# Sums of W_out built during the first pair's output projection, and one form of the branch kept in DRAM

## The chip, the cores and the metric

The kernel runs on one core of a Trainium2 chip. Its engines work side by side, each through its own list of instructions and strictly in that order: TensorE (PE, with its weight loads as PEld), VectorE (DVE), ScalarE (ACT), GpSimd (POOL) and SyncE (SP), which here only issues DMAs. POOL and ScalarE can issue DMAs too. The metric is the device time in microseconds; less is better.

## The reference

One layer of an encoder trunk over 2048 rows of 1024 numbers, in fp32. Cut to what matters here:

```python
hn = rms_norm(h, norm_g[i])
proj = jnp.einsum('bsd,de->bse', hn, pool_w_in[j])
u, mq, gate = jnp.split(proj, [POOL_WIDTH, POOL_WIDTH + MEM_WIDTH], axis=-1)
tok = multi_scale_pool(u, w_group[j], scale[j])
mem_o = memory_attention(mq, mem_k, mem_v)
branch = jnp.concatenate([tok, mem_o], axis=-1) * jax.nn.silu(gate)
h = h + jnp.einsum('bse,ed->bsd', branch, w_out[i])
return rms_norm(h, final_norm_g)
```

## The kernel before, in words

The rows are handled in two pairs of blocks, 1024 rows each; pair 0 first. Each pair goes through an input projection (queries, gates, pooled columns, with the attention to the memory spread between the products) and an output projection. Every matrix product of fp32 numbers is made of three matmuls on a high part and a low part (`_mm3`, L51 to L53): `_split` (L42) makes the parts, the high one by a cast on ScalarE (L38), the low one by a subtraction on VectorE (L46). `chunk` (L411) does this for weights, into a ring of four buffers `wh` and `wl`.

Pair 1 uses seven products of quarter matrices in place of eight, in both projections. So sums and differences ("forms") of quarters are needed: of its inputs (X1), of its branch (Y, seven forms) and of W_out (four forms, 5, 6, 7 and 4).

- `stage_weights(k)` (L702), for k = 0 to 3, makes the sums of W_out: four loads of 256 KB, four subtractions on VectorE (`combine`, L241, whose operations are recorded at L102), and four stores of 256 KB to `t_d` by POOL's queue (L714). Before, it works in three `zz` buffers (a ring of four that the queries and the pooling use as well) and an `sg` buffer, loads by SP (L708), and is called inside the second pair's input projection, `project_in(1)`, after products 12, 26, 30 and 34 of its 56.
- `stage_branch(k)` (L674) makes the forms of pair 1's branch: it loads two pieces of the branch (`load_branch`, L645: from `br_d`, or, for the attention's, from `o_d` with its gate from `g_d`, multiplied at L655), adds and subtracts on VectorE (L102, L105), and either splits a form into its slots (Y) or stores it to `ys_d` (L690). Its buffers are `raw`, a ring of four that the weight chunks use as well. It is called in `project_out(0)`, the first pair's output projection, at the chunks (dh, c) = (0, 2), (0, 3), (1, 0) and (1, 1).
- `y_later(p)` (L694) loads a stored form again and splits it into slots.
- `project_out(0)` (L774): for each half dh of the columns, four chunks c of W_out (load at L780, 512 KB), 48 matmuls each into eight PSUM banks; after the half, `Rows.complete` (L744) adds the banks into h on VectorE (L742).
- `project_out_by_products` (L802): seven products of 48 matmuls, in the order 1, 2, 6, 7, 5, 4, 3; products 5, 6, 7 and 4 load their weights from `t_d` (L817).

Large slots x0 to x13 (`slot`, L84) hold X1, the split branch of pair 0 and Y in turn, one tile at a time; a new tile of a slot waits for every use of the old one. x6 and x7 hold form 4 of X1 during `project_in(1)`, and form 6 of Y after it.

The listing sets the rank of each instruction; a planner that runs a model of time then orders each engine's list by rank and by when buffers and operands come free in that model. So loads of a later stage can be issued well before the stage, and an instruction on the chip waits at the place in the list that the planner gave it. What it waits for is set by the tiles: POOL's, SP's and ScalarE's DMAs wait in their engine's list.

Of the kernel before, what the change touches and what calls it, by code (L numbers as in the profile page):

```python
# [8 lines left out]
F32 = mybir.dt.float32  # L9
# [6 lines left out]
P = 128  # L16
# [3 lines left out]
KH = KT // 2  # L20
BT = 512
# [35 lines left out]
def trunk(ctx, tc, x, xT, mem, memT, norm_g, mem_norm_g, w_mem, w_out, w_in, w_uT, w_g, p_scale, final_g,  # L57
# [5 lines left out]
    nc = tc.nc  # L63
    sp = nc.sync
# [8 lines left out]
    sgp = pool("sgp", 2)  # L73
# [5 lines left out]
    dram = pool("dram", 1, space=bass.MemoryType.DRAM)  # L79
# [4 lines left out]
    def slot(n, shape=(P, KH, BT), dt=F32R):  # L84
        return sl.tile(list(shape), dt, name=f"x{n}")

    def zz(shape, dt=F32):

        n = 1
        for v in shape[1:]:  # L90
            n *= v
        t = zw.tile([P, HALO + D], dt, name="zz")[:, :n]
        if len(shape) == 3:
            t = t.rearrange("p (a b) -> p a b", a=shape[1])
        return t
# [566 lines left out]


    YPLACE = {1: (2, 3), 2: (4, 5), 6: (6, 7), 7: (8, 9), 5: (10, 11), 4: (12, 13), 3: (0, 1)}
    ys_d = dram.tile([KH, P, 4, BT], F32, name="ys_d")
    t_d = dram.tile([4, 2, P, 2, BT], F32, name="t_d")
    LATER = (7, 5, 4, 3)
    FORMS = (5, 6, 7, 4)
    Y = {}

# [2 lines left out]

    def stage_branch(k):  # L674
        if not Y:
            for p in (1, 2, 6):
                y_slots(p)
        r = [load_branch(1, e, lambda: raw_tile((P, 2, BT))) for e in (k, k + KH)]
        a11, a21, a12, a22 = r[0][:, 0, :], r[0][:, 1, :], r[1][:, 0, :], r[1][:, 1, :]
        t = raw_tile((P, 2, BT))  # L680
        s1, s2 = t[:, 0, :], t[:, 1, :]
        s4 = st.tile([P, BT], F32, name="s")
        g = nc.vector
        add(g, s1, a21, a22)
        sub(g, s2, s1, a11)
        sub(g, a21, a11, a21)
        sub(g, s4, a12, s2)
        for p, v in {1: a11, 2: a12, 6: s2, 7: a21, 5: s1, 4: a22, 3: s4}.items():
            if p in LATER:
                sp.dma_start(out=ys_d[k, :, LATER.index(p), :], in_=v)  # L690
            else:
                _split(nc, Y[p][0][:, k, :], Y[p][1][:, k, :], v, "act")

    def y_later(p):  # L694
        y_slots(p)
        for k in range(0, KH, 2):
            rt = raw_tile((P, 2, BT))
            sp.dma_start(out=rt, in_=ys_d[k:k + 2, :, LATER.index(p), :].rearrange("k p t -> p k t"))
            for kk in range(2):
                _split(nc, Y[p][0][:, k + kk, :], Y[p][1][:, k + kk, :], rt[:, kk, :], "act")  # L700

    def stage_weights(k):  # L702

        r = []
        for kk in (k, k + KH):
            r.append(zz((P, 2, BT)))
            for dh in range(2):
                sp.dma_start(out=r[-1][:, dh, :], in_=w_out[kk // 2, dh, :, kk % 2, :])  # L708
        t = zz((P, 2, BT))
        t4 = sgp.tile([P, BT], F32, name="sg")  # L710
        b11, b12, b21, b22 = r[0][:, 0, :], r[0][:, 1, :], r[1][:, 0, :], r[1][:, 1, :]
        combine(b11, b12, b21, b22, t[:, 0, :], t[:, 1, :], t4)
        for i, v in enumerate((t[:, 0, :], t[:, 1, :], b12, t4)):
            nc.gpsimd.dma_start(out=t_d[i, k // 2, :, k % 2, :], in_=v)  # L714
# [59 lines left out]
    def project_out(s, bh, bl, between):  # L774
        rows = Rows(s)
        for dh in range(2):
            pss = [pl.tile([P, BT], F32, name=n) for pl, n in [(ps_mm, "mm")] * 4 + [(ps_s, "sc")] * 2 + [(ps_t, "pt")] * 2]
            for c in range(4):
                wr = raw_tile((P, 2, BT))
                sp.dma_start(out=wr, in_=w_out[c, dh])  # L780
                ws = [chunk(wr[:, kk, :], "act") for kk in range(2)]
                if dh == 0 and c == 2:
                    rows.load()
                between(dh, c)

                rounds = [[(kk, t)] for kk in range(2) for t in range(NT)]
                if c == 3:
                    rounds = [[(kk, t) for kk in range(2)] for t in range(NT)]
                for todo in rounds:
                    for kk, t in todo:  # L790
                        e = 2 * c + kk
                        tk = slice(t % QT * P, (t % QT + 1) * P)
                        ah, al = bh[t // QT, e // KH], bl[t // QT, e // KH]
                        _mm3(nc, pss[t], ah[:, e % KH, tk], al[:, e % KH, tk], ws[kk][0], ws[kk][1], e == 0, e == KT - 1)
            for t in range(NT):
                added = rows.complete(t, dh, pss[t])
                if dh and t:
                    with tc.issue_after(added.ins):
                        rows.finish(t - 1)
        rows.finish(NT - 1)  # L800

    def project_out_by_products():  # L802
        rows = Rows(1)
        banks = {}

        def product(p, onto=None, tile_by_tile=False, each=None):
            if onto:
                banks[p] = banks[onto]
            elif p == 1:
                banks[p] = [ps_mm.tile([P, BT], F32, name="mm") for _ in range(QT)]  # L810
            else:
                banks[p] = [pl.tile([P, BT], F32, name=n) for pl, n in ((ps_s, "sc"), (ps_t, "pt")) for _ in range(2)]
            ws = []
            for c in range(2):
                wr = raw_tile((P, 2, BT))
                if p in FORMS:
                    sp.dma_start(out=wr, in_=t_d[FORMS.index(p), c])  # L817
                else:
                    sp.dma_start(out=wr, in_=w_out[c + 2 * (p > 1), int(p == 3)])
                ws += [chunk(wr[:, kk, :], "act") for kk in range(2)]  # L820
            order = [(k, t) for k in range(KH) for t in range(QT)]
            if tile_by_tile:
                order = [(k, t) for t in range(QT) for k in range(KH)]
            for k, t in order:
                tk = slice(t * P, (t + 1) * P)
                _mm3(nc, banks[p][t], Y[p][0][:, k, tk], Y[p][1][:, k, tk], ws[k][0], ws[k][1], k == 0 and not onto,
                     k == KH - 1, skip_group_check=onto is not None)
                if tile_by_tile and k == KH - 1:
                    each(t)

        def all_tiles(p, f, t0, dh):
            for t in range(QT):
                f(t0 + t, dh, banks[p][t])

        product(1)
        rows.load()
        all_tiles(1, rows.add, 0, 0)
        product(2)
        all_tiles(2, rows.complete, 0, 0)
        y_later(7)  # L840
        product(6, 1)
        all_tiles(6, rows.add, QT, 0)
        y_later(5)
        product(7)
        all_tiles(7, rows.add, QT, 1)
        y_later(4)
        product(5, 6)
        all_tiles(5, rows.complete, QT, 1)
        y_later(3)
        product(4, 7)  # L850
        for t in range(QT):
            added = rows.complete(QT + t, 0, banks[4][t])
            if t:
                with tc.issue_after(added.ins):
                    rows.finish(QT + t - 1)
        rows.finish(2 * QT - 1)

        def last(t):
            added = rows.complete(t, 1, banks[5][t])
            if t:  # L860
                with tc.issue_after(added.ins):
                    rows.finish(t - 1)
        product(3, 5, True, last)
        rows.finish(QT - 1)
# [46 lines left out]
    def norm(a):  # L911
        first_norm(a)
        for f in unscaled[a]:
            f()

    hooks = {7: [lambda: norm(0)], 10: [lambda: norm(1)], 11: [load_fold] * 4 + [lambda: loaded.extend(load_memory())],
             12: [fold, lambda: ahead.append(load_tile(w_in[6], load))],
             14: [lambda: load_memory_rest(loaded)],
             15: [lambda: memory_norm(loaded)], 17: [lambda: memory(loaded)], 19: [lambda: stats(0)], 21: [lambda: stats(1)]}
# [23 lines left out]
    bhl = [({}, {}), ({}, {})]  # L943
# [11 lines left out]
            branch(s, e, *bhl[s], lambda: (zz if by == "zz" else raw_tile)((P, 2, BT)))  # L955

    hooks = {NP - 4: [lambda: bring(0, 0, (0, 1, 2, 3), "zz")], NP - 2: [lambda: bring(0, 1, (4, 5, 6, 7), "zz")]}
    for k, n in enumerate((12, 26, 30, 34)):
        hooks[n] = [lambda k=k: stage_weights(k)]
    project_in(1, X1, Steps(1, 10, 2, hooks))  # L960

    AT_CHUNK = {(0, 2): 0, (0, 3): 1, (1, 0): 2, (1, 1): 3}
    project_out(0, *bhl[0], lambda dh, c: stage_branch(AT_CHUNK[dh, c]) if (dh, c) in AT_CHUNK else None)
    project_out_by_products()


# [47 lines left out]
```

## Time and profile before

| | us |
|---|---|
| median of 3 runs | 629.32 (629.0 to 629.76) |
| the profiled execution | 627.59 |
| its span, first to last instruction | 625.8 |
| TensorE busy | 590.5 |
| VectorE busy | 450.7 |
| DMA | 144.34 MB, 231 GB/s on average |

The profile is one execution. Its views tell: the busy time of each engine; who waited for whom; the instructions of an engine in order of time, with the idle time before each in square brackets and what ended it; the same summed by stretches of time, with the granted clock of TensorE (1.00 is 2.4 GHz, 0.50 is 1.2 GHz), the share of the 16 DMA engines in use and the rate; and the DMAs by line with the time from issue to landing. Times in the rows are microseconds from the span's start unless they are marked ns. The second pair's input projection runs from about 230 to 456 us, the first pair's output projection from 446 (the two overlap a little) to 539 us, the seven products from there to 617 us.

### The profile page before, as it was taken

The page shows a single profiled execution, that of the slowest core. Times are in us where ns is not written, and L with a number is a line of the kernel's source. Part 1 is how long each engine was busy: PE and PEld are TensorE (multiplying, and loading weights), DVE is VectorE, ACT ScalarE, POOL GpSimd, SP SyncE. Part 2 cuts the span into 40 slices and gives each one's busy share as a digit, 9 for nine tenths or more (in the row PEclk, how much of TensorE's full clock was granted, in tenths as well). Part 3 has the DMA queues.
Part 4 walks back from the last instruction along what each step waited for, and adds up shares of the span by engine and source line. Part 5 has one row for each costly group of instructions (what it writes and reads, how often), then busy time and mean ns, then how long its engine had stood idle before and what let it go on. Part 6 is the DMA issues. An engine that isn't in the chain of part 4 may idle for free. (4 is left out here: it accounts for less than half of the span.)

```text
span 625.8 us, 8556 instructions
## 1 busy us (share of the span) xinstructions
PE 590.5 (94%) x2798; PEld 489.0 (78%) x2798; DVE 450.7 (72%) x754; ACT 347.5 (56%) x707; POOL 160.3 (26%) x182
## 2 busy tenths in 40 slices
PE   7989989998999999999998899989999999999994
PEld 4879778876887878887886688868788888887883
DVE  6460446789888647896789878798894842969775
ACT  6835545445467584666763779734552512516454
POOL 0052133355251304001048212264100000304053
PEclk8999999999899999999999989989999999999997
DMA  8989994477385435758341986335999574698606
GB/s 317 399 331 333 345 318 135 134 225 266 133 291 206 155 132 170 235 193 283 137 127 55 303 272 229 127 129 197 344 376 349 160 257 140 238 364 326 230 18 251
DMA packets 62799, 144.34 MB, mean 231 GB/s; under 512 B 7714, under 2 KB 16674, under 8 KB 62756
## 3 DMA queue, kind: packets, MB, share of 16 engines
q1 hardware_dynamic: 52468, 120.20, 57.1%
q10 hardware_dynamic: 6832, 12.60, 5.3%
q0 software_dynamic: 3456, 11.01, 4.6%
q8 instruction: 22, 0.36, 0.2%
q14 instruction: 21, 0.17, 0.1%
HBM read 98.17 MB, written 45.09 MB: 229 GB/s over the span
## 5 line engine op out<-in xcount | busy, mean ns | idle before, releaser
L51 PE MATMUL mm<-x,wh 128*128 128x512 f32 x480 | 190.4, 399 | 4.4 <-ACT x L229 1.8
L52 PE MATMUL mm<-x,wh 128*128 128x512 f32 x480 | 190.2, 397 | 0.3 <-DVE x L230 0.3
L53 PE MATMUL mm<-x,wl 128*128 128x512 f32 x480 | 189.1, 398 | 1.1 <-DVE wl L46 1.1
L46 DVE TENSOR_TENSOR wl<-raw,wh 128x512 fp32r<-128x512 f32 x116 | 92.6, 804 | 63.1 <-ACT wh L38 62.8
L530 POOL TENSOR_TENSOR zz<-zz 128x527 f32<-128x527 f32 (+6 forms) x64 | 82.7, 1303 | 116.4 <-DVE zz L557 47.8
L38 ACT CAST wh<-raw 128x512 fp32r<-128x512 f32 x116 | 70.7, 619 | 72.0 <-PE pt L53 21.8
L51 PEld LDWEIGHTS mm<-x,wh 128*128 128x128 f32 x480 | 91.7, 191 | 23.9 <-ACT x L229 2.3
L53 PEld LDWEIGHTS mm<-x,wl 128*128 128x128 f32 x480 | 91.8, 191 | 19.7 <-DVE wl L46 1.5
L52 PEld LDWEIGHTS mm<-x,wh 128*128 128x128 f32 x480 | 91.7, 191 | 18.4 <-DVE x L230 0.6
L52 PE MATMUL mm<-wl,x 128*128 128x512 f32 x128 | 49.8, 389 | 0.0
L53 PE MATMUL mm<-wh,x 128*128 128x512 f32 x128 | 49.8, 389 | 0.0
L51 PE MATMUL mm<-wh,x 128*128 128x512 f32 x128 | 46.8, 390 | 1.1 <-ACT wh L38 1.1
L595 ACT ACTIVATE pr<-sc,nm 128x256 f32<-128x256 f32 x64 | 29.8, 471 | 32.3 <-DVE nm L591 32.1
L600 ACT ACTIVATE pr<-pr,rc 128x256 f32<-128x256 f32 x64 | 29.1, 503 | 30.4 <-DVE rc L598 30.2
L38 ACT CAST x<-raw 128x512 fp32r<-128x512 f32 x40 | 24.0, 619 | 36.0 <-DMA raw<-ys_d 12.6
L760 POOL TENSOR_TENSOR rstdo<-sso,half 128x1 f32<-128x1 f32 x16 | 13.2, 839 | 114.3 <-DVE sso L752 114.3
L46 DVE TENSOR_TENSOR x<-raw,x 128x512 fp32r<-128x512 f32 x40 | 29.6, 755 | 7.6 <-ACT x L38 7.6
L51 PEld LDWEIGHTS mm<-wh,x 128*128 128x128 f32 x128 | 24.0, 188 | 6.5 <-ACT wh L38 1.5
L53 PEld LDWEIGHTS mm<-wh,x 128*128 128x128 f32 x128 | 24.0, 188 | 5.0
L52 PEld LDWEIGHTS mm<-wl,x 128*128 128x128 f32 x128 | 24.0, 188 | 5.0
L611 PE MATMUL pt<-ident,pr 128*128 128x128 f32 x128 | 22.0, 286 | 5.6 <-ACT pr L600 5.4
L46 DVE TENSOR_TENSOR ptl<-pt,pth 128x512 fp32r<-128x512 f32 x32 | 21.8, 680 | 5.5 <-ACT pth L38 5.3
(189 smaller groups left out, 1065.1 us busy)
## 6 DMA issues: line engine op xcount, KB each, us to landing
raw<-in_w_in SPq DMA_DIRECT2D x19, 512.0 KB, 5.5
x<-in_x SPq DMA_DIRECT2D x16, 512.0 KB, 8.8
g_d<-sg ACTq DMA_DIRECT2D x32, 256.0 KB, 4.6
raw<-in_w_out SPq DMA_DIRECT2D x14, 512.0 KB, 4.6
raw<-w_z SPq DMA_DIRECT2D x12, 512.0 KB, 5.0
sg<-g_d SPq DMA_DIRECT2D x24, 256.0 KB, 3.3
br_d<-zz SPq DMA_DIRECT2D x12, 512.0 KB, 3.4
x<-in_xT SPq DMA_DIRECT2D x8, 512.0 KB, 6.7
```

The costliest lines, as they stand in the source:

```text
L38: return nc.scalar.copy(hi, src)
L46: return e.tensor_tensor(out=lo, in0=src, in1=hi.bitcast(F32), op=ALU.subtract)
L51: nc.tensor.matmul(ps, lhsT=ahi, rhs=bhi, start=start, stop=False, **kw)
L52: nc.tensor.matmul(ps, lhsT=ahi, rhs=blo, start=False, stop=False, **kw)
L53: nc.tensor.matmul(ps, lhsT=alo, rhs=bhi, start=False, stop=stop, **kw)
L530: nc.gpsimd.tensor_tensor(out=cur[rows, c0:c1], in0=prev[rows, c0:c1], in1=prev[rows, c0 - step:c1 - step], op=ALU.add)
L595: nc.scalar.activation(out=pr[:, h, :], in_=ps[:, h, :], func=AF.Exp, bias=nm[:, h:h + 1], accum_out=su[:, h:h + 1])
L600: nc.scalar.mul(pr[:, h, :], pr[:, h, :], rc[:, h:h + 1])
L611: nc.tensor.transpose(ps[:, 2 * h + kt, :], pr[:, h, kt * P:(kt + 1) * P], ident)
L760: nc.gpsimd.tensor_tensor(out=ro, in0=self.sso[:, 1, t:t + 1], in1=half[:, :1], op=ALU.pow)
```

## The change

`stage_weights` is called in `project_out(0)` in place of `project_in(1)`: at the chunks (0, 3), (1, 0), (1, 1) and (1, 2), right behind `stage_branch` where both are called. It works in the slots x6 and x7 (two tiles in place of three `zz` and an `sg`), and its loads are issued by POOL instead of SP. Since these slots are then not free for form 6 of Y during this stage, form 6 is no longer split in `stage_branch` but stored to `ys_d`, like forms 7, 5, 4 and 3, and is loaded and split by `y_later(6)`, listed after product 1.

```diff
--- before.py
+++ after.py
@@ -662,9 +662,9 @@
 
 
     YPLACE = {1: (2, 3), 2: (4, 5), 6: (6, 7), 7: (8, 9), 5: (10, 11), 4: (12, 13), 3: (0, 1)}
-    ys_d = dram.tile([KH, P, 4, BT], F32, name="ys_d")
+    ys_d = dram.tile([KH, P, 5, BT], F32, name="ys_d")
     t_d = dram.tile([4, 2, P, 2, BT], F32, name="t_d")
-    LATER = (7, 5, 4, 3)
+    LATER = (6, 7, 5, 4, 3)
     FORMS = (5, 6, 7, 4)
     Y = {}
 
@@ -673,7 +673,7 @@
 
     def stage_branch(k):
         if not Y:
-            for p in (1, 2, 6):
+            for p in (1, 2):
                 y_slots(p)
         r = [load_branch(1, e, lambda: raw_tile((P, 2, BT))) for e in (k, k + KH)]
         a11, a21, a12, a22 = r[0][:, 0, :], r[0][:, 1, :], r[1][:, 0, :], r[1][:, 1, :]
@@ -701,13 +701,12 @@
 
     def stage_weights(k):
 
-        r = []
-        for kk in (k, k + KH):
-            r.append(zz((P, 2, BT)))
+        b, t = (slot(n, (P, 2, 2, BT), F32) for n in YPLACE[6])
+        r = [b[:, i] for i in range(2)]
+        for kk, v in zip((k, k + KH), r):
             for dh in range(2):
-                sp.dma_start(out=r[-1][:, dh, :], in_=w_out[kk // 2, dh, :, kk % 2, :])
-        t = zz((P, 2, BT))
-        t4 = sgp.tile([P, BT], F32, name="sg")
+                nc.gpsimd.dma_start(out=v[:, dh, :], in_=w_out[kk // 2, dh, :, kk % 2, :])
+        t, t4 = t[:, 0], t[:, 1, 0, :]
         b11, b12, b21, b22 = r[0][:, 0, :], r[0][:, 1, :], r[1][:, 0, :], r[1][:, 1, :]
         combine(b11, b12, b21, b22, t[:, 0, :], t[:, 1, :], t4)
         for i, v in enumerate((t[:, 0, :], t[:, 1, :], b12, t4)):
@@ -835,6 +834,7 @@
         product(1)
         rows.load()
         all_tiles(1, rows.add, 0, 0)
+        y_later(6)
         product(2)
         all_tiles(2, rows.complete, 0, 0)
         y_later(7)
@@ -955,12 +955,16 @@
             branch(s, e, *bhl[s], lambda: (zz if by == "zz" else raw_tile)((P, 2, BT)))
 
     hooks = {NP - 4: [lambda: bring(0, 0, (0, 1, 2, 3), "zz")], NP - 2: [lambda: bring(0, 1, (4, 5, 6, 7), "zz")]}
-    for k, n in enumerate((12, 26, 30, 34)):
-        hooks[n] = [lambda k=k: stage_weights(k)]
     project_in(1, X1, Steps(1, 10, 2, hooks))
 
-    AT_CHUNK = {(0, 2): 0, (0, 3): 1, (1, 0): 2, (1, 1): 3}
-    project_out(0, *bhl[0], lambda dh, c: stage_branch(AT_CHUNK[dh, c]) if (dh, c) in AT_CHUNK else None)
+    def sums(dh, c):
+        n = 4 * dh + c
+        if 2 <= n < 6:
+            stage_branch(n - 2)
+        if n >= 3 and n < 7:
+            stage_weights(n - 3)
+
+    project_out(0, *bhl[0], sums)
     project_out_by_products()
```

## Rows read from the trace of the kernel before

**Rows 1.** The page's first section: busy time, share of the span, instructions

```profile
PE 590.5 (94%) x2798; PEld 489.0 (78%) x2798; DVE 450.7 (72%) x754; ACT 347.5 (56%) x707; POOL 160.3 (26%) x182
```

**Rows 2.** TensorE's waits, 227 to 450 us: total us, times, longest

```profile
PE pt L611 <- ACT pr L600: 3.7, 2, 2.4
PE sc L623 <- DVE ptl L46: 2.4, 1, 2.4
```

**Rows 3.** VectorE in time: start, us, line, op, tiles [idle before <-releaser]

```profile
353.12 0.69 DVE L102 TENSOR_TENSOR zz<-zz 128x512 f32<-128x512 f32 x1 [1.79 <-DMA zz<-in_w_out]
353.73 0.68 DVE L46 TENSOR_TENSOR wl<-s,wh 128x512 fp32r<-128x512 f32 x1
...
355.63 1.29 DVE L102 TENSOR_TENSOR zz<-zz 128x512 f32<-128x512 f32 x2 [0.61 <-DMA zz<-in_w_out]
356.95 0.69 DVE L591 TENSOR_REDUCE nm<-sc 128x2 f32<-128x512 f32 x1
```

**Rows 4.** ScalarE in order of time, around 350 us

```profile
349.24 0.62 ACT L38 CAST wh<-s 128x512 fp32r<-128x512 f32 x1
...
354.11 1.28 ACT L595 ACT_TABLE_LOAD   x1
```

**Rows 5.** TensorE in order of time, the two waits

```profile
354.46 0.50 PE L53 MATMUL mm<-x,wl 128*128 128x512 f32 x1 [1.10 <-DVE wl L46]
...
358.75 0.39 PE L588 MATMUL sc<-khi,mq 128*128 128x256 f32 x1 [1.62 <-ACT pr L595]
```

**Rows 6.** Stretches: us, busy (x) by engine, PEclk, DMA share, GB/s

```profile
359.57:362.98 3.41, 3.41 (x8) 2.70 (x9) 2.94 (x6) 2.88 (x5) 0.11 (x1) 0.50 0.96 287
```

**Rows 7.** DMA issues, 340 to 390 us: KB each, median us to landing

```profile
zz<-in_w_out SPq DMA_DIRECT2D x12, 256.0 KB, 5.3
t_d<-zz POOLq DMA_DIRECT2D x9, 256.0 KB, 4.6
raw<-w_z SPq DMA_DIRECT2D x4, 512.0 KB, 4.9
```

**Rows 8.** Groups by line, 280 to 392 us: busy us, mean ns, idle

```profile
L102 DVE TENSOR_TENSOR zz<-zz 128x512 f32<-128x512 f32 x12 | 7.9, 689 | 6.5 <-DMA zz<-in_w_out 6.4
...
L714 POOL DMA_DIRECT2D t_d<-zz x12 | 6.5, 545 | 58.1 <-DVE zz L102 57.7 <-DVE rc L598 0.3
```

**Rows 9.** Stretches; engines in order PE, PEld, DVE, ACT, POOL

```profile
410.00:420.00 10.00, 7.56 (x37) 5.96 (x36) 9.96 (x12) 3.90 (x10) 6.86 (x7) 0.88 0.36 111
456.00:480.00 24.00, 24.00 (x108) 19.87 (x107) 20.02 (x33) 11.30 (x20) 0.00 (x0) 1.00 0.99 370
480.00:490.00 10.00, 10.00 (x46) 8.29 (x45) 4.49 (x9) 3.62 (x8) 0.00 (x0) 1.00 0.73 268
490.00:500.00 10.00, 10.00 (x46) 8.28 (x45) 9.47 (x21) 5.90 (x16) 0.00 (x0) 1.00 0.47 136
500.00:510.00 10.00, 10.00 (x46) 8.29 (x45) 4.59 (x8) 1.87 (x3) 0.00 (x0) 1.00 0.66 220
510.00:530.00 20.00, 20.00 (x90) 16.57 (x89) 5.47 (x9) 3.54 (x6) 0.00 (x0) 1.00 0.54 191
...
540.00:550.00 10.00, 10.00 (x45) 8.28 (x45) 10.00 (x20) 4.86 (x12) 3.43 (x4) 1.00 0.87 298
```

**Rows 10.** TensorE in order of time: X1's last matmul, chunk (1, 2)'s first

```profile
455.74 0.39 PE L53 MATMUL mm<-x,wl 128*128 128x512 f32 x1
...
517.16 0.39 PE L51 MATMUL mm<-wh,x 128*128 128x512 f32 x1
```

**Rows 11.** SP's queue in order of time

```profile
507.80 0.38 SPq L780 DMA_DIRECT2D raw<-in_w_out  x1
```

**Rows 12.** VectorE in order of time, the last gate and the chunk

```profile
506.06 1.29 DVE L655 TENSOR_TENSOR raw<-raw 128x512 f32<-128x512 f32 x2 [2.30 <-DMA raw<-g_d]
...
513.15 1.29 DVE L46 TENSOR_TENSOR wl<-raw,wh 128x512 fp32r<-128x512 f32 x2 [2.05 <-ACT wh L38]
```

**Rows 13.** DMA issues, 450 to 480 us

```profile
zz<-o_d SPq DMA_DIRECT2D x2, 512.0 KB, 7.2
```

## The prediction

> **What bounds the kernel now.** I read the busy row of TensorE first: it is busy 94% of the span [rows 1], so time can only come out of what TensorE waits for, out of a lower clock, or out of the two ends. The second view, TensorE's own waits in the second pair's input projection, has few entries; the two largest stand in [rows 2], and two smaller ones, which matter here, are seen one by one below. From 456 us on, in every stretch shown up to 550 us, TensorE has no idle time at all [rows 9], so the output projections are bound by TensorE, as long as what feeds it keeps its lead. That is the frame: **time can be won where the sums of W_out are taken away, and lost where they are put.**
>
> Third view, VectorE in order of time around 350 us [rows 3]. VectorE takes its instructions in their listed order. Before 353.12 us it stands 1.79 us at a sum of `stage_weights(1)`, whose load has not landed. Behind it is the `wl` part of a weight chunk (L46, at 353.73), whose high part ScalarE had ready by 349.86 us [rows 4]. TensorE waits for that `wl`, 1.10 us [rows 5]. The next two sums wait 0.61 us more for their loads, and behind them, at 356.95, is the maximum L591 of an attention step [rows 3]. ScalarE's exponentials (L595), and then TensorE, wait for it: 1.62 us [rows 5]. So both stalls are named after L46 and L595, but what holds VectorE's queue is a sum that waits for its own DMA.
>
> Fourth, the clock: after these two pauses it stands at half (1.2 GHz) from 359.57 to 362.98 us [rows 6].
>
> **The change, part by part.**
>
> *Taken out of the input projection.* Sixteen sums on VectorE: 12 of 689 ns [rows 8] and the four that write `t4`, of the same shape; 11.0 us in a stage where TensorE is the bound, worth nothing by themselves. They are worth something where TensorE waited behind them: 1.10 + 1.62 us [rows 5], and the slow clock after them, 3.41 us at half speed or 1.7 us of lost work [rows 6]. **Sum: 4.4 us.** What is late next there: without the sums that `wl` can start at 351.33 (353.12 less the 1.79 of idle time) and ends at 352.0, 2.4 us before TensorE gets it now; L591 follows the next `wl` at about 354, three us sooner. A table load of ScalarE (1.28 us, to 355.4 us [rows 4]) stands ahead of the exponentials, which then still come over 2 us sooner than now. The bound below is nothing (the order on VectorE is made anew, and another operation may stand in the same place); the bound above is the 4.4 plus the stall of 2.4 us at 415 us [rows 2], should it go as well. I take 4.4, since the rows show both stalls behind sums. The sums of k = 0, 2 and 3 lie elsewhere and no stall of TensorE follows them: nothing. The 16 loads also leave SP's queue, where no wait of TensorE names them, and three buffers `zz` at a time are freed, which POOL alone might want, with cover.
>
> *Put into the first pair's output projection.* The two slots x6 and x7 hold X1's form 4 until the last of its products, at 455.74 us [rows 10]; W(0)'s loads start there, since POOL has nothing else from 456 to 530 us [rows 9]. POOL's 32 issues of 545 ns [rows 8], 17 us, are hidden by that. From there it is a chain through one pair of slots: four loads (5.3 us to landing), four sums (2.8 us), four stores (4.6 us), then the next k [rows 7, 8]. With 3 us of issuing that is 15 to 17 us a turn, so four turns end at 516 to 524 us. The sums must be stored before product 6 (about 560 us), and the slots be free before form 6 is split (from 520 us on): cover of 35 us, and some. On VectorE 11 us come on top of what it does; it has idle time in each stretch from 456 to 530 [rows 9], and TensorE's `wl` parts lie several us ahead there, so a sum that stands 1 to 3 us for its load, as in [rows 3], is covered, *unless* it delays the chain below.
>
> *The chain with the least cover.* `stage_branch` runs through four `raw` buffers: loads of k+1 wait for the stores of k, and the W_out chunk of (dh, c) = (1, 2) waits for the buffer of the last gate. In the trace: VectorE stands 2.30 us for that gate's load, to 506.06 [rows 12], and only after its products does SP issue the chunk's load, at 507.80 [rows 11]. The chunk's first `wl` is written by about 513.8 (the first of two in 1.29 us from 513.15 [rows 12]); TensorE starts the chunk at 517.16 [rows 10]. **Cover: 3.3 us.**
>
> What lengthens this chain is DMA. From 456 to 480 us the engines' share is 0.99 at 370 GB/s, from 480 to 490 it is 0.73 [rows 9]. By 490 us W has moved loads of k = 0, stores of k = 0 and loads of k = 1: 3.1 MB, at 370 GB/s 8.5 us, into 24 us with 0.2 us free and 10 us with 2.7 free: 5.6 us pushed back. From 490 to 510 the share is 0.47 and 0.66, 8.7 us free [rows 9], and W wants some 6: 0 to 2.6 us (one load of 1 MB in its way); I take 0.7. Form 6 adds four stores of 0.26 MB, 0.7 us each, and takes away four casts and four subtractions of the same size: nought. Against it: the turn of k = 2 now falls into the stretch with VectorE at 9.47 of 10 us (the sums into h of the first half) and would come out of it into one at 4.59 [rows 9]; I count 2.3 us back for that. So the chain comes 4 us later, **0.7 us beyond the cover**. Bounds: 0, and 5.6 + 2.6 + 1.5 for sums that stand in VectorE's queue, less 3.3: 6.4 us.
>
> A rule that speaks against this part: the Trainium skill, "DMA: Bandwidth & Descriptors", section "Issuing engines are not separate DMA queues", says that DMAs begun by SP, ScalarE or GpSimd run on the same 16 engines, and that another issuer saves only the sequencer's time. The share of 0.99 agrees that nothing is left there for a new queue. Had POOL's queue been a path of its own, the 5.6 us would be nought and the sum 0.7 us better.
>
> *Form 6 through DRAM.* It is stored in `stage_branch` (counted) and comes back after product 1 in the listing: two loads of 0.5 MB, four casts, four subtractions. VectorE has 5.47 us of work in the 20 us from 510 to 530 [rows 9], so its 2.8 us fit, and the `raw` buffers are free again before products 2 and 7 want them. If the slots come late, the work falls past 530, where VectorE is full (10.00 of 10 from 540 to 550 [rows 9]). Between 0 and 2.8 us; I take 0.8.
>
> **Sum.** -4.4 + 0.7 + 0.8 = -2.9 us. The profiled execution took 627.59 us (span 625.8 and 1.8 around it), the runs' median is 629.32; the difference is laid on the median: **626.4 us**. Its own range, by the bounds of the small terms, is 624.5 to 628.
>
> **Rivals.**
>
> *Contention eats it (slower).* The chain comes 9.7 us later, chunk (1, 2) stalls TensorE by 6.4 us, and the clock falls after that pause as it did at 359.57 [rows 6], 1.7 us more: 629.3 - 4.4 + 6.4 + 1.7 = 633.0; with two thirds of that delay some 631. It decides from the point where the chain is about 7 us late (3.3 of cover, then what is left of the 4.4). For it: the share of 0.99, and landing times of 7.2 us from 450 to 480 [rows 13] where transfers of the same 0.5 MB took 4.9 earlier [rows 7]. Against: W's chain is slow itself, and most of its traffic falls after 490 us. The same page of the Trainium skill, in "Queues, rings and completion order", says that each engine goes round between the rows that have work. By it SP's backlog moves at half speed while W's is in flight, which makes this rival likelier; no row before the change shows POOL's queue beside a full SP queue.
>
> *The won time is taken by the next wait (no change).* A new order puts another late operation ahead of `wl`, only half of the 4.4 us comes, and 1.5 to 2 us are lost later: 628.9. For it: TensorE's wait of 2.4 us for `ptl` [rows 2], at 341 us, has no sum near it, and is of this kind.
>
> *More than that.* With everything from 353 us on earlier, the stall before L611 at 415 us goes too: 2.4 us [rows 2] and the slow clock behind it (0.88 in these ten us, as far as they reach [rows 9]), together about 4 us: 622.4. Against: VectorE is at 9.96 of 10 there without any sum in it [rows 9].
>
> *It does not do what it says.* W(3) ends only after 540 us, the products wait for it, and ScalarE stands at form 6's casts with product 1's later chunks behind them. It would take turns of 21 us instead of 15 to 17; some 631.
>
> **How the numbers follow.** Forecast 0.40, contention 0.24, no change 0.20, more 0.12, late slots 0.04. Faster by over 0.2% (1.3 us, about what a measurement of this kernel can tell from none) are nearly all of the first, the fourth and little of the third: 0.54. Within 0.2%: 0.18. Slower: 0.28. The range leaves out the far ends of contention and of "more": 622.8 to 632.2.
>
> **What would show it.** Right: from 345 to 365 us no wait of TensorE for `wl` or L595 and no half clock; W's loads from POOL at about 452 us; the load of chunk (1, 2) issued some 4 us later against the chunk's place on TensorE. Contention: landing times of 8 us and more from 456 to 500 us, and TensorE waiting for `wh` or `wl` behind `raw<-in_w_out`. Wrong altogether if the input projection shows as much idle TensorE as before, or if TensorE stalls for the sums into h.

## The result and the profile after

The changed kernel takes 633.78 us (median of 11 runs, 631.88 to 637.39) against 629.32 us for the kernel before, measured beside it: a ratio of 1.0083, 95% interval 1.006 to 1.0106. It is slower; 626.4 was forecast, and 633.78 lies beyond the range. The profiled execution took 633.53 us, its span is 631.8.

TensorE has as much work as before [rows 1], in a longer span. The page's first section of the kernel after:

```profile
PE 590.7 (94%) x2798; PEld 489.6 (78%) x2798; DVE 451.1 (71%) x754; ACT 348.2 (55%) x707; POOL 172.9 (27%) x198
```

I cut each span at places that all kernels have. A is the end of TensorE's last wait for an attention step before 230 us, up to which the kernels of the table run one and the same list. h1 and h2 are the first sums into h of the two halves of `project_out(0)`. From h1 to h2 lie four chunks' worth of matmuls; with TensorE never idle and at full clock that is 43.5 us. The names of the experiments are told further down; all times are us from each profiled execution, so a difference between two rows is one of single executions: up to A, where nothing was edited, they already differ by 2.6 us.

| kernel | start to A | A to h1 | h1 to h2 | h2 to last matmul | rest | span |
|---|---|---|---|---|---|---|
| before | 227.1 | 259.0 | 43.5 | 87.2 | 9.0 | 625.8 |
| after | 225.9 | 254.9 | 52.6 | 87.7 | 10.7 | 631.8 |
| e1, form 6 alone | 227.4 | 262.6 | 43.5 | 85.6 | 8.9 | 628.0 |
| e4, one load in four | 226.8 | 253.4 | 50.2 | 85.8 | 9.2 | 625.4 |
| e5, no W at all | 224.8 | 255.6 | 43.5 | 86.2 | 8.6 | 618.6 |
| e9, W late | 226.9 | 255.7 | 45.2 | 106.2 | 8.9 | 643.0 |
| e11, in place | 224.9 | 256.6 | 43.5 | 86.5 | 8.9 | 620.4 |

So in these two traces the second pair's input projection gave back 4.1 us and the first pair's output projection lost 9.1. The loss is firm: with no wait at chunk (1, 2), the stretch from h1 to h2 is 43.5 us in before, e1, e5 and e11 alike. The gain is there, but its size is not firm: e1, whose listing of the input projection is that of before, took 262.6 us from A to h1 in place of 259.0, and the eight kernels without W's sums there (the four of the table, e2, e3, e6, e7) took 253.0 to 256.9. That makes 2.1 to 9.6 us. TensorE's waits of after show both. First from 227 to 450 us, where the wait for L600 of 2.4 us [rows 2] is gone as well and the one for L105 has come; then from 450 us to the end (columns: who, waited for whom, total, times, longest):

```profile
PE mm L51 <- DVE u L105: 3.0, 2, 2.8
PE sc L623 <- DVE ptl L46: 2.4, 1, 2.4
PE pt L611 <- ACT pr L600: 0.3, 1, 0.3
...
PE mm L51 <- ACT wh L38: 6.9, 1, 6.9
PE sc L51 <- ACT wh L38: 1.1, 1, 1.1
PE sc L52 <- DVE wl L46: 0.5, 1, 0.5
```

The 6.9 us are the first matmul of chunk (1, 2). TensorE, ScalarE and SP of after in order of time (columns as in [rows 10, 11]) tell how it came about:

```profile
518.96 0.80 PE L51 MATMUL mm<-wh,x 128*128 128x512 f32 x1 [6.93 <-ACT wh L38]
...
508.76 0.62 ACT L38 CAST x<-raw 128x512 fp32r<-128x512 f32 x1 [7.97 <-DMA raw<-br_d]
...
518.28 1.14 ACT L38 CAST wh<-raw 128x512 fp32r<-128x512 f32 x2 [5.12 <-DMA raw<-in_w_out]
...
513.51 0.45 SPq L779 DMA_DIRECT2D raw<-in_w_out  x1
```

Read from below: SP issues the chunk's load at 513.51, where TensorE has already run dry at 512.02 (518.96 less 6.93). Before, the load went out 9.4 us ahead of TensorE [rows 10, 11]. ScalarE stood 7.97 us for a piece of the branch (`raw<-br_d`) that `stage_branch` was waiting for. Behind the wait TensorE's clock drops, and 2.1 us more are lost (5.04 us of work at 0.57); with the 6.9 that is the 9.1 of the table. The stretches of after, to be laid beside [rows 9] (the sixth number after the engines' busy times is the clock, then the share of the DMA engines and GB/s):

```profile
456.00:480.00 24.00, 24.00 (x108) 19.87 (x107) 17.32 (x28) 6.75 (x12) 4.33 (x8) 1.00 1.03 414
480.00:490.00 10.00, 10.00 (x46) 8.29 (x45) 6.95 (x16) 5.56 (x15) 0.54 (x1) 1.00 0.89 332
490.00:500.00 10.00, 10.00 (x46) 8.29 (x45) 7.52 (x14) 2.65 (x7) 3.79 (x7) 1.00 0.67 235
500.00:510.00 10.00, 10.00 (x46) 8.29 (x45) 2.57 (x4) 1.41 (x3) 0.54 (x1) 1.00 0.91 343
510.00:530.00 20.00, 13.07 (x50) 10.35 (x50) 11.82 (x20) 3.52 (x6) 5.65 (x11) 0.83 0.85 317
516.00:524.00 8.00, 5.04 (x14) 4.07 (x15) 2.23 (x4) 1.14 (x2) 1.39 (x3) 0.57 1.01 373
```

No stretch has less than 0.67 of the DMA engines in use, where before there were 0.73, 0.47 and 0.66. What that does to a transfer, in the view of DMA issues from 456 to 510 us, the first two lines of before, the others of after:

```profile
DMA packets 5347, 15.13 MB, mean 280 GB/s; under 512 B 605, under 2 KB 605, under 8 KB 5345
raw<-br_d SPq DMA_DIRECT2D x4, 512.0 KB, 5.1
...
DMA packets 6644, 19.04 MB, mean 353 GB/s; under 512 B 909, under 2 KB 909, under 8 KB 6642
raw<-br_d SPq DMA_DIRECT2D x4, 512.0 KB, 9.8
q0 software_dynamic: 1642, 5.35, 25.6%
```

The branch's pieces, on which `stage_branch` stands, take 9.8 us to land in place of 5.1. A quarter of the engines' time goes to q0, POOL's queue, which carries W.

### The profile page after: what moved, and what is told of

Same layout as the page of the kernel before. It is cut to its first block, busy times and chain, and to the rows that moved or that the text cites. A ratio compares the mean times of both kernels' runs of the same rounds, so it can differ in the third digit from the quotient of the medians.

```text
span 631.8 us, 8569 instructions
## 1 busy us (share of the span) xinstructions
PE 590.7 (94%) x2798; PEld 489.6 (78%) x2798; DVE 451.1 (71%) x754; ACT 348.2 (55%) x707; POOL 172.9 (27%) x198
## 4 chain that ended last, share of the span: by engine, by line
PE 49%; DVE 20%; DMA 10%; ACT 10%; issue 7%; POOL 2%; SPq 0%; ACTq 0%; POOLq 0%; DVEq 0%
PE mm L51 12%; PE mm L52 12%; PE mm L53 12%; DVE wl L46 3%; DMA raw<-in_xT 3%; DMA raw<-t_d 3%; DVE x L46 2%; DVE zz L545 2%; ACT pr L595 2%; DMA raw<-br_d 2%; ACT L595 2%; ACT wh L38 2%; PE sc L53 2%; DVE zz L539 1%; PE pt L53 1%
## 5 line engine op out<-in xcount | busy, mean ns | idle before, releaser
L46 DVE TENSOR_TENSOR wl<-raw,wh 128x512 fp32r<-128x512 f32 x116 | 90.3, 787 | 58.5 <-ACT wh L38 58.0
L530 POOL TENSOR_TENSOR zz<-zz 128x527 f32<-128x527 f32 (+6 forms) x64 | 84.0, 1325 | 163.9 <-ACT zz L555 77.1
L53 PEld LDWEIGHTS mm<-x,wl 128*128 128x128 f32 x480 | 91.7, 191 | 18.1
L52 PEld LDWEIGHTS mm<-x,wh 128*128 128x128 f32 x480 | 91.4, 190 | 18.4 <-DVE x L230 0.6
L600 ACT ACTIVATE pr<-pr,rc 128x256 f32<-128x256 f32 x64 | 29.0, 502 | 26.5 <-DVE rc L598 26.3
L38 ACT CAST x<-zz 128x512 fp32r<-128x512 f32 x32 | 18.3, 618 | 18.6 <-DVE zz L655 7.0
L611 PE MATMUL pt<-ident,pr 128*128 128x128 f32 x128 | 22.0, 286 | 3.7 <-ACT pr L600 3.6
L591 DVE TENSOR_REDUCE nm<-sc 128x2 f32<-128x512 f32 x32 | 21.7, 682 | 4.7 <-PE sc L589 4.5
```

The source lines that it names most:

```text
L38: return nc.scalar.copy(hi, src)
L46: return e.tensor_tensor(out=lo, in0=src, in1=hi.bitcast(F32), op=ALU.subtract)
L52: nc.tensor.matmul(ps, lhsT=ahi, rhs=blo, start=False, stop=False, **kw)
L53: nc.tensor.matmul(ps, lhsT=alo, rhs=bhi, start=False, stop=stop, **kw)
L530: nc.gpsimd.tensor_tensor(out=cur[rows, c0:c1], in0=prev[rows, c0:c1], in1=prev[rows, c0 - step:c1 - step], op=ALU.add)
L591: nc.vector.tensor_reduce(out=nm, in_=ps, axis=AX.X, op=ALU.max, negate=True)
```

## The experiments

`stage_branch` has four turns; the first sum of each on VectorE (L105, `raw<-raw`) marks it. In the table: the three distances between these marks, the load of chunk (1, 2) counted from h1, and TensorE's wait there. Without a wait TensorE is at that chunk 31.1 us after h1. W's bytes are those moved in this stage.

| kernel | W's loads, stores, MB | turns, us | load after h1 | wait |
|---|---|---|---|---|
| before | 0, 0 | 15.8, 16.1, 14.7 | 21.7 | none |
| e1, form 6 alone | 0, 0 | 17.6, 17.4, 13.0 | 21.3 | none |
| e5, no W at all | 0, 0 | 15.1, 16.4, 13.5 | 20.4 | none |
| e9, W late | 0, 0 until the load | 15.4, 15.7, 13.7 | 20.7 | none |
| after | 4.2, 4.2 | 20.0, 18.9, 18.4 | 32.7 | 6.9 |
| e7, loads by SP | 4.2, 4.2 | 21.3, 17.4, 18.5 | 32.9 | 6.7 |
| e3, no sums | 4.2, 4.2 | 22.5, 17.4, 20.0 | 35.3 | 7.7 |
| e6, no stores | 4.2, 0 | 20.0, 17.5, 18.1 | 31.6 | 5.4 |
| e4, one load in four | 1.0, 4.2 | 20.4, 18.7, 15.8 | 30.0 | 3.7 |

**e1: form 6 through DRAM, alone.** The kernel before with the `ys_d`, `LATER` and `y_later(6)` lines of the change and nothing else:

```diff
-    LATER = (7, 5, 4, 3)
+    LATER = (6, 7, 5, 4, 3)
...
-            for p in (1, 2, 6):
+            for p in (1, 2):
...
+        y_later(6)
         product(2)
```

> The kernel before with form 6 alone sent through DRAM; the sums of W_out stay in the input projection. Theory A (the 8 MB of W's loads and stores, moved into the first pair's output projection, lengthen the turns of stage_branch, and the load of chunk (1, 2) hangs on the last turn): only 2 MB more here, the chain at most 2 us later against a cover of 3.3 us, TensorE does not wait at that chunk; 629 to 630 us, within 0.3% of the kernel before. Theory C (it is form 6's store: the buffer that it leaves comes free only when the store has landed): the load of chunk (1, 2) goes out 3 us or more later than at 507.8, and the time is 631 to 634.

Measured: 629.88 us, ratio 1.0025 (0.9996 to 1.0053). No wait at chunk (1, 2), and the load comes 21.3 us after h1. That is theory A: the four stores of form 6 don't delay the chain against TensorE (the first two turns are 1.3 to 1.8 us longer, the third 1.7 shorter).

**e3: the transfers without the sums.**

```diff
-        combine(b11, b12, b21, b22, t[:, 0, :], t[:, 1, :], t4)
-        for i, v in enumerate((t[:, 0, :], t[:, 1, :], b12, t4)):
+        for i, v in enumerate((b11, b21, b12, b22)):
```

> The changed kernel without the sixteen subtractions that make the sums of W_out: the loaded pieces are stored as they are (the four forms are left out, so the products work on wrong weights); all of W's transfers stay, on the same queue, through one slot. Theory A (transfers): the load of chunk (1, 2) is as late as in the changed kernel, TensorE waits 5 to 8 us there, 632 to 635 us. Theory B (W's sums stand in VectorE's list, wait for their loads and hold back the additions of stage_branch): the wait is below 2 us, 625 to 627 us.

Measured: 633.2 us, ratio 1.01 (1.0048 to 1.0153). The wait is there in full, with a second one of 1.5 us ahead of it, at chunk (1, 1). So the sums in VectorE's list are not what makes it (theory B falls). Without them W's loads do not even keep step with the turns of `stage_branch`, whose marks are at 454.7, 477.2, 494.6 and 514.6 us: W's loads go out at 450.00, 468.19 and then (POOL of e3 in order of time)

```profile
486.14 2.17 POOL L708 DMA_DIRECT2D x<-in_w_out  x4 [6.11 <-DMA t_d<-x]
498.40 2.17 POOL L708 DMA_DIRECT2D x<-in_w_out  x4 [3.48 <-DMA t_d<-x]
```

and the turns of `stage_branch` are at least as long as in after (59.9 us for the three, 57.4).

**e4: the same sums and stores, with W loaded for k = 0 alone.**

```diff
+        if not W:
+            W.extend(slot(n, (P, 2, 2, BT), F32) for n in YPLACE[6])
+        b, t = W
...
-            for dh in range(2):
+            for dh in range(2 if k == 0 else 0):
```

> The changed kernel with the pieces of W_out loaded for k = 0 alone; the other three rounds take their sums from what the round before left (so these forms are wrong), with all sixteen subtractions and all sixteen stores. 3 MB less to move between 470 and 524 us. Theory A: about half of what delays the turns is gone, the wait at chunk (1, 2) is 0 to 3 us, 626 to 629.5 us. Theory B: sums as many as before, but none waits for a load any more; B as a matter of the sums' own 11 us says 632 us and more, with the wait above 5 us.

Measured: 627.71 us, ratio 0.9988 (0.9963 to 1.0013). Three MB less shorten the wait to 3.7 us (theory A had 0 to 3), the third turn most (15.8).

**e2: each chunk of W_out loaded one chunk earlier.**

```diff
-                wr = raw_tile((P, 2, BT))
-                sp.dma_start(out=wr, in_=w_out[c, dh])
+                for n in range(len(wrs), min(4 * dh + c + 2, 8)):
+                    wrs.append(raw_tile((P, 2, BT)))
+                    sp.dma_start(out=wrs[n], in_=w_out[n % 4, n // 4])
+                wr = wrs[4 * dh + c]
```

> The changed kernel, with each chunk of W_out of the first pair's output projection loaded one chunk earlier, ahead of the stage_branch listed there; the same bytes, sums and queues. If the lost time is only that chunk (1, 2) hangs on the last turn of stage_branch through the four raw buffers (A, B and C all say so), the wait of 6.9 us and the slow clock of 1.7 us behind it go, the turns themselves stay as slow: 624 to 626 us, below the kernel before. If TensorE would have waited for something else late in that chain (the split forms of the branch, stored forms), the wait moves to the products: 630 us and more.

Measured: 635.74 us, ratio 1.013 (1.0097 to 1.0163). The first answer is missed, the second came true: the wait moves. The load of chunk (1, 2) is now out at 500.20 us, but a buffer given to it early is taken from the turns, and the last one falls later still. TensorE's waits of e2 from 460 us to the end, and a stretch of it where VectorE has no idle time left (15.00 of 15.00):

```profile
PE sc L52 <- DVE wl L46: 3.2, 2, 2.1
PE sc L51 <- ACT wh L38: 1.6, 1, 1.6
PE mm L52 <- DVE wl L46: 1.4, 1, 1.4
PE mm L51 <- ACT wh L38: 1.1, 1, 1.1
...
545.00:560.00 15.00, 12.91 (x50) 10.17 (x49) 15.00 (x27) 3.42 (x6) 4.60 (x3) 0.89 1.03 401
```

One wait became five, at chunk (1, 3) and in the products after it. The place of the buffer only decides where the late turns are felt.

**e5: no W at all.** What is left of the change is form 6 and the empty place in the input projection:

```diff
-                    sp.dma_start(out=wr, in_=t_d[FORMS.index(p), c])
+                    sp.dma_start(out=wr, in_=w_out[c + 2, 0])
...
-        if n >= 3 and n < 7:
-            stage_weights(n - 3)
```

> The changed kernel without any sums of W_out (no loads, sums or stores of them, neither in the input projection nor in the first output projection); products 5, 6, 7 and 4 read pieces of W_out in their place, so the output is not the layer's. Form 6 goes through DRAM. Theory 1 (W's traffic alone makes the wait at chunk (1, 2), through stage_branch's chain): the chain follows TensorE, which comes some 4 us earlier, the chunk's load leads its first matmul by about 9 us as in the kernel before, no wait there, 624 to 625.5 us. Theory 2 (the chain is bound by DMA on its own and does not follow TensorE, so that the 4 us won in the input projection are themselves taken out of the cover): the load is issued near 507 to 509 us on the clock of the span, the lead falls to 4 to 6 us, TensorE waits 0 to 2 us, 625.5 to 627.5 us.

Measured: 621.31 us, ratio 0.9856 (0.98 to 0.9912). The chain follows TensorE, and the load leads by 10.7 us (31.1 less 20.4): theory 1. The time is 2.7 us below its range; of the profiled execution's gain 2.3 us lie ahead of A, where nothing was edited, and the rest of the surplus is not explained. The marks of the four turns on VectorE and the chunk's load on SP, first of e5, then of after (one more mark, the first, is at 455.79 us):

```profile
455.50 0.69 DVE L105 TENSOR_TENSOR raw<-raw 128x512 f32<-128x512 f32 x1
470.56 0.69 DVE L105 TENSOR_TENSOR raw<-raw 128x512 f32<-128x512 f32 x1 [0.49 <-DMA raw<-br_d]
486.96 0.68 DVE L105 TENSOR_TENSOR raw<-raw 128x512 f32<-128x512 f32 x1
500.43 0.69 DVE L105 TENSOR_TENSOR raw<-raw 128x512 f32<-128x512 f32 x1
500.80 0.42 SPq L779 DMA_DIRECT2D raw<-in_w_out  x1
...
475.82 0.69 DVE L105 TENSOR_TENSOR raw<-raw 128x512 f32<-128x512 f32 x1 [1.58 <-DMA raw<-br_d]
494.75 0.69 DVE L105 TENSOR_TENSOR raw<-raw 128x512 f32<-128x512 f32 x1
513.14 0.69 DVE L105 TENSOR_TENSOR raw<-raw 128x512 f32<-128x512 f32 x1
```

Both start together; after falls behind by 5.3, 7.8 and 12.7 us. Two stretches of e5, to be held against those of after: from 480 to 490 the share is 0.52 in place of 0.89.

```profile
456.00:480.00 24.00, 24.00 (x108) 19.88 (x107) 15.54 (x26) 7.70 (x14) 0.00 (x0) 1.00 0.99 379
480.00:490.00 10.00, 10.00 (x46) 8.29 (x45) 8.72 (x19) 5.38 (x14) 0.00 (x0) 1.00 0.52 160
```

**e6: loads and sums, no stores.**

```diff
-        for i, v in enumerate((t[:, 0, :], t[:, 1, :], b12, t4)):
-            nc.gpsimd.dma_start(out=t_d[i, k // 2, :, k % 2, :], in_=v)
```

> The changed kernel with the loads and sums of W_out in place, but without their 16 stores (4 MB); products 5, 6, 7 and 4 read pieces of W_out instead, so the output is not the layer's. If the bytes on the DMA engines make the delay, whichever way they go, taking away 4 MB of stores does a little more than taking away 3 MB of loads did (wait of 3.7 us at chunk (1, 2) there): wait 2 to 3.5 us, 626 to 627.5 us. If the loads alone delay the chain (stores come when nothing waits), the wait stays at 6 to 7 us and the time at 632 to 634.

Measured: 629.16 us, ratio 1.0001 (0.9971 to 1.0032), between the two answers: the wait falls to 5.4 us. So in the traces stores count too, but less than loads, and neither alone accounts for the delay. The times of e4 and e6 don't tell the two apart: their intervals overlap. Against the load at 32.7 us after h1, leaving out three of four loads saves 2.7 us, leaving out the stores 1.1, leaving out everything 12.3.

**e7: W's loads on SP's queue.**

```diff
-                nc.gpsimd.dma_start(out=v[:, dh, :], in_=w_out[kk // 2, dh, :, kk % 2, :])
+                sp.dma_start(out=v[:, dh, :], in_=w_out[kk // 2, dh, :, kk % 2, :])
```

> The changed kernel with the loads of W_out issued by SP's queue in place of POOL's, all bytes and all sums as in the changed kernel. If the DMA engines are the limit whoever issues: the loads of stage_branch still land in 8 to 10 us, wait of 5 to 8 us at chunk (1, 2), 632 to 635 us. If POOL's queue, going round beside SP's, is what halves the speed of SP's loads: SP's loads then come in listed order, ahead of the sums' loads, the wait falls below 4 us, under 630 us. If SP stands at the loads of W (which wait for slots) with loads of the branch behind them: worse than 634 us.

Measured: 631.17 us, ratio 1.0013 (0.9985 to 1.0041), between the two answers in time, with the wait as the first had it. The waits at chunk (1, 2) of e3 (two waits), e4, e6 and e7, in this order, from the view of TensorE's waits:

```profile
PE mm L51 <- ACT wh L38: 9.3, 2, 7.7
PE mm L51 <- ACT wh L38: 3.7, 1, 3.7
PE mm L51 <- ACT wh L38: 5.4, 1, 5.4
PE mm L51 <- ACT wh L38: 6.7, 1, 6.7
```

Who issues the loads doesn't change the wait: 6.7 us by SP, 6.9 by POOL. The Trainium skill's "DMA: Bandwidth & Descriptors", section "Issuing engines are not separate DMA queues", by which all of them run on the same DMA engines, agrees with that. That two queues of loads share the engines by turns, as the Trainium skill has it in the same page's "Queues, rings and completion order", is not needed for the delay: with W's loads in SP's own queue the turns are as long (57.2 us for the three, 57.4 in after). W's stores stayed in POOL's queue, so that two queues have some part in it is not excluded. Why e7's time is nevertheless below that of after (the intervals of the two ratios don't meet) is open: its profiled execution is the slowest of its ten, 633.56 us, and shows no such gain.

**e9: all of W queued behind the load of chunk (1, 2).** As e7, and:

```diff
+                with tc.issue_after(held[6].ins):
+                    sp.dma_start(out=v[:, dh, :], in_=w_out[kk // 2, dh, :, kk % 2, :])
...
-                sp.dma_start(out=wr, in_=w_out[c, dh])
+                held.append(sp.dma_start(out=wr, in_=w_out[c, dh]))
```

`stage_weights` is called for all k at chunk (1, 3).

> The changed kernel with all loads of W_out's sums on SP's queue and queued behind the load of chunk (1, 2), so that none of their 8 MB moves while stage_branch's chain still has a load to make. Theory (their bytes delay that chain): the chunk's load leads TensorE again by 9 us or more, no wait at chunk (1, 2), first half of the output projection 43.5 us from its first to its second set of sums into h. But the sums then end late (four turns of 14 to 17 us from about 502 us: 558 to 570), product 6's weights come late, and TensorE waits for them, some 3 to 15 us: 625 to 637 us. If the wait at chunk (1, 2) stays at 5 us or more, it is not the bytes.

Measured: 643.91 us, ratio 1.0214 (1.0168 to 1.026). As expected in kind, but 7 us beyond the upper end in time: with W's bytes out of the way the turns take 15.4, 15.7 and 13.7 us, and no wait stands at chunk (1, 2) (the 45.2 us of the first table are a late sum on VectorE, TensorE has no pause there). The price is paid later. TensorE's waits of e9 from 480 us on:

```profile
PE mm L51 <- ACT x L38: 12.1, 1, 12.1
PE sc L51 <- ACT wh L38: 4.0, 1, 4.0
```

The 12.1 us, at 564.5 to 576.6, are form 6, whose slots W holds too long. In the slots x6 and x7 these 8 MB have no good place: early they delay the branch, late they delay form 6.

**e8, e10, e11, e12: leave the sums where they were, and mend them there.** After e5 the gain to be had in the input projection was plain. e8 makes the sums in place (b11 is overwritten by b12 - b11, and so on), in two `zz` buffers in place of three and an `sg`; it also loads two products earlier, and lists the sums three products behind their loads. e10 is this distance alone, with the old buffers, e11 the sums in place alone, listed where they were, e12 is e8 with a distance of five. The edit of e11:

```diff
-        t = zz((P, 2, BT))
-        t4 = sgp.tile([P, BT], F32, name="sg")
...
-        combine(b11, b12, b21, b22, t[:, 0, :], t[:, 1, :], t4)
-        for i, v in enumerate((t[:, 0, :], t[:, 1, :], b12, t4)):
+        g = nc.vector
+        sub(g, b11, b12, b11)
+        sub(g, b12, b22, b12)
+        sub(g, b22, b22, b11)
+        sub(g, b21, b21, b22)
+        for i, v in enumerate((b11, b22, b12, b21)):
```

> The kernel before (sums of W_out in the second pair's input projection, form 6 split at once), with the sums made in place in two zz buffers in place of three and an sg, their loads issued two products earlier than before and each set of sums listed three products behind its loads and behind the latest low part of a weight chunk. Theory (the two stalls of TensorE at 354 and 359 us come from sums that wait for their own load ahead of a low part): both stalls go, nothing is put into the first output projection, chunk (1, 2) keeps a lead of 8 us or more: 624.5 to 626.5 us. Rival (the order made anew puts another wait there, or the buffers held longer make the queries wait): 628 to 630 us.

> The kernel before, sums of W_out in the second pair's input projection in their old buffers (three zz and an sg), but loads two products earlier and sums listed three products behind their loads and behind the latest low part of a weight chunk. If the distance between load and sum makes the gain of the in-place version (0.99 of the time before): 622 to 626 us. If the gain comes from holding fewer zz buffers: 627 us or more.

> The kernel before with the sums of W_out made in place (two zz buffers in place of three and an sg), listed where they were, products 12, 26, 30 and 34. If holding fewer buffers makes the gain: 622 to 626 us. If the distance does: 627 to 630 us, with waits of TensorE behind sums near 354 us as in the kernel before.

> The in-place version with its sums five products behind their loads in place of three. There a sum still held VectorE for 2.9 us to 349.3 us, and TensorE for 2.3 us behind it. If distance is what counts: that wait goes, 621 to 624 us. If the zz buffers held longer delay queries and pooling: 625 us or more.

Measured: e8 623.63 us, ratio 0.9895 (0.9845 to 0.9944); e10 628.77, 0.999 (0.9958 to 1.0022); e11 623.66, 0.99 (0.9861 to 0.9938); e12 626.12, 0.9928 (0.9898 to 0.9958). Distance does nothing measurable with the old buffers, and two products more of it, in e12, do not help (the second answer came true). The sums in place take 1% off, and my reason for e8 falls. The wait behind a sum is even still there in e11, where a sum holds VectorE for 3.03 us (TensorE in order of time, then the stretch behind it):

```profile
352.69 0.50 PE L53 MATMUL mm<-x,wl 128*128 128x512 f32 x1 [2.42 <-DVE wl L46]
...
353.00:356.50 3.50, 3.50 (x17) 2.86 (x16) 2.96 (x6) 3.09 (x5) 0.54 (x1) 1.00 1.03 352
```

e11 beats both kernels. What in it saves the time is not settled. Its profiled execution is 2.4 us shorter from A to h1; 2.2 us more lie ahead of A, where its list is that of before, and are no part of the edit.

## Why the prediction was wrong, step by step

**The gain in the input projection: near in sum, not in its terms.** 4.4 us were forecast, 4.1 are measured from A to h1 in one trace each, and by the other traces it may be 2.1 to 9.6. That the number fits is in part luck. The two waits of 1.10 and 1.62 us [rows 5] are gone. The 1.7 us of slow clock behind them [rows 6] did not come back: the slow stretch moved to 342 us, behind the 2.4 us wait for `ptl`, which is in both kernels [rows 2]. In its place two small waits went that the sum left out: 0.5 us at 285.9 us of before and 1.1 us at 445.2. The wait of 2.4 us before L611 [rows 2] did not go, as the rival "more than that" had it, but gave way to one of 2.8 us, for L105, a microsecond later in the span.

**Form 6 and the small terms.** 0.8 us were taken for form 6; e1 bounds it at -0.25 us to 3.3 us (0.9996 to 1.0053), and its span from h2 to the last matmul is shorter than that of before (85.6 us, 87.2). Not more can be said.

**The failed step: the delay of the chain, 4 us, 0.7 beyond its cover.** The mechanism was right, the size of its term was not. The right chain was named, with its end (load of chunk (1, 2), then `wh`), but its delay was 11.0 us against TensorE (32.7 less 21.7), and 6.9 us of that came through. The cover was 4.1 us by that, not 3.3: the prediction counted to the first `wl`, but the chunk's first matmul reads `wh`, whose cast ends in before at 513.11 us, 4.05 ahead of it. ScalarE of before:

```profile
512.49 0.62 ACT L38 CAST wh<-raw 128x512 fp32r<-128x512 f32 x1 [2.55 <-DMA raw<-in_w_out]
```

The terms of the 4 us, one by one, against the turns of before:

- 5.6 us for W's bytes up to 490: the first two turns became longer by 4.2 and 2.8, 7.0 us. The method, bytes over rate less free time, was near.
- 0.7 us (of 0 to 2.6) from 490 to 510: the third turn became 3.7 us longer. Free time of 8.7 us for 6 us of transfers was taken for room. But a turn does not use the mean of a stretch, it stands for its own transfers one after the other. In the second turn of after SP stands 2.6 us for a store of the branch before it can issue the first load, which goes out 6.2 us after the mark (3.6 in before). In the third that load goes out 3.5 us after the mark (5.9 in before), but takes 10.4 us to land, where it took 3.8. SP's wait and that load, after:

```profile
SPq L649 <- DMA ys_d<-raw: 2.6, 1, 2.6
...
raw<-br_d SPq DMA_DIRECT2D x1, 512.0 KB, 10.4
```

- "Most of its traffic falls after 490 us", the reason given against contention, was worked out from turns of W that run free, 15 to 17 us. They were 21.8, 22.5 and 19.1 us. POOL in order of time, after:

```profile
451.35 2.19 POOL L708 DMA_DIRECT2D x<-in_w_out  x4 [14.16 <-PE mm L53]
473.13 2.17 POOL L708 DMA_DIRECT2D x<-in_w_out  x4 [6.65 <-DMA t_d<-x]
495.59 2.17 POOL L708 DMA_DIRECT2D x<-in_w_out  x4 [1.84 <-DMA t_d<-x]
514.67 2.17 POOL L708 DMA_DIRECT2D x<-in_w_out  x4 [1.93 <-DMA t_d<-x]
```

  Each set of W's loads starts here within 5 us of a mark of `stage_branch` (455.8, 475.8, 494.8, 513.1). That the two chains run in step is not what makes the delay: in e3, and in e6, whose sums stand in VectorE's list as in after, they are out of step by up to 16.2 and 13.5 us, and the waits are 7.7 and 5.4 us.
- 2.3 us back, for the turn of k = 2 coming out of a stretch full of sums into h: nothing of it is left in the turn. What its loads won at the start, 2.4 us, went at their landing: VectorE stood 6.18 us for the branch's high part, which waited for `raw<-br_d`.

That the parts don't add up (2.7 us for loads, 1.1 for stores, 12.3 for all) fits this reading: a turn that waits for its own stores and then for its own loads is held by either kind that lies beside it. The second and the third turn of after show one of each kind; that it explains the sums is argued, not shown by a run.

**The rivals.** "Contention eats it", at 0.24, is what happened: 6.4 us of wait were set down for it against 6.9 measured, 1.7 of slow clock against 2.1, 633.0 us against 633.78. Its price was the upper bound of the step that failed (5.6 + 2.6 + 1.5 less the cover), though the 1.5 for sums in VectorE's queue is no part of it (e3). That the 4 us won earlier eat the cover by themselves (theory 2 of e5) falls with e5. "It does not do what it says" had its condition in after, turns of 21 us, but not its price: W's last store is issued at 529.77 us, and TensorE waits no more than 1.1 and 0.5 us behind it. The price was paid only in e9.

**The range** ended at 632.2, since the far end of contention was left out. In hindsight, by the two signs in its favour, a share of 0.99 and landing times that had risen to 7.2 us already [rows 9, 13], it deserved to be the likeliest case.

## What to carry to other kernels

Before you move transfers to where "DMA has room", follow the chain with the least cover turn by turn: count each of its landings at the latency of a full machine (here 5.1 us became 9.8), not the free share of a stretch times its length. A second chain of transfers beside it lengthens its turns, in step with it (after) or not (e3), and by whichever queue its loads go (e7). And where sums load an engine or hold buffers in a tight stage, try first to make them in place: here that took 1% off, with nothing moved, though why is not settled.

## What the hardware did that was not expected

**The clock did not fall at each pause of one length.** TensorE waits 2.35 us for `ptl` in before, and 2.36 and 2.35 in after and e5, at the same instruction. Behind it, TensorE in order of time and the stretch that follows, first of after, then of e5, then the stretch of before (its wait ends at 343.89 us):

```profile
340.95 0.39 PE L623 MATMUL sc<-ptl,vhl 128*128 128x256 f32 x1 [2.36 <-DVE ptl L46]
342.00:345.50 3.50, 3.50 (x12) 2.91 (x11) 3.50 (x6) 1.87 (x7) 2.30 (x2) 0.52 0.97 321
...
340.83 0.39 PE L623 MATMUL sc<-ptl,vhl 128*128 128x256 f32 x1 [2.35 <-DVE ptl L46]
340.80:344.30 3.50, 3.47 (x21) 3.08 (x22) 3.50 (x6) 1.79 (x4) 2.45 (x3) 1.00 0.99 297
...
344.00:347.40 3.40, 3.40 (x21) 3.02 (x22) 3.40 (x5) 1.81 (x5) 2.06 (x2) 1.00 0.94 320
```

After falls to 1.2 GHz (0.52), e5 and before stay at 2.4 GHz (1.00). A term "slow clock behind this wait" of 1.7 us is thus no sure gain when the wait goes, and can appear at a wait that was harmless. Executions of one list differ in it too: from 0 to 224 us, where before and e5 run the same, the clock is 0.98 and 1.00, and A comes 2.3 us sooner in e5.

**The DMA engines gave more than the stage before had shown.** From 456 to 480 us after moved 414 GB/s at a share of 1.03, before 370 at 0.99 [rows 9]. The estimate of 5.6 us was made with 370; with W's transfers beside the branch's the rate was higher, while the branch's pieces took 9.8 us in place of 5.1 to land.

**A rest that varies.** From TensorE's last matmul to the end of the span it is 8.6 to 9.2 us in most kernels, but 10.7 in after, 10.6 in e2 and 10.2 in e3. The last store is issued 4.7 us after the last matmul in before and in after; the 1.6 us lie behind it and are left open.
